# Seven block products instead of eight in four last blocks, with GpSimd making low parts of streamed operands

## The chip, the cores and the metric

The kernel runs on one core of one Trainium2 chip. The metric is the device time of one execution, in microseconds; lower is better. TensorE (PE) multiplies matrices, VectorE (DVE), ScalarE (ACT) and GpSimd (POOL) work on tiles, and SyncE (SP) issues most DMA transfers.

## What is computed

One layer of a streaming encoder on a sequence of 2048 tokens of width 1024, in float32: token mixing, cross-attention into 256 memory tokens, and a dense SwiGLU feed-forward with 2816 hidden channels, each between root-mean-square norms and with a residual. The part around the change is the last:

```python
u = rms_norm(h, g_ffn_pre[l])
y = (jax.nn.silu(u @ w_gate[l]) * (u @ w_up[l])) @ w_down[l]
h = h + rms_norm(y, g_ffn_post[l])
```

## The kernel before, in words

Every float32 factor is split into a high part (a copy rounded to the matmul's type `F32R`) and a low part (the rest), and a product of two factors is three matmuls: high by high, high by low, low by high (`products`, lines 1122 to 1124). `split2` makes the two parts: ScalarE (line 985) or GpSimd (line 987) copies the high part, VectorE subtracts to get the low part (line 988).

The large products after the mixing are a list of jobs (`jobs`, line 1411), run one after the other by `phases` (line 1210): the output projection, the two products of the cross-attention, the feed-forward for the first and for the second half of the tokens (22 blocks each: gate and up in turn), and the down projection in three jobs of 8 blocks over 6, 8 and 8 of the 22 hidden tiles. A job has one *resident* factor, kept in SBUF for all its blocks, and a *streamed* factor that is loaded per block. Each block is a 2 x 2 block matrix product. Kind `s` does it in seven block products in Strassen's manner (`seven`, steps 1, 5, 6, 3, 7, 2, 4), kind `p` in eight plain ones (`eight`, resident blocks 1, 2, 8, 3, two products each). A block product is 3 x nk matmuls of 128 x 512; nk is 4, and 3 in the first down job. In the seven-product form the resident factor comes as seven tiles (blocks and sums of blocks; the sums are made ahead and lie in DRAM as `u_s` and `d_s`), and the streamed factor as seven operands of 128 x 512, four of them sums made by VectorE (`combine`, line 1097). Products 1, 5 and 6 of a block are copied out of PSUM by ScalarE (`copy`, line 1137) and added to later ones by VectorE in the block's `out`.

SBUF has seven places for resident tiles (`slots` in `phases`: four called A, three called B). A resident tile is made in two halves, each loaded into one of nine row buffers (`row_tile`, line 1453; `half` issues the load) and split two steps later (`split`: ScalarE the high part, VectorE the low part; these instructions are queued behind the last ScalarE and VectorE work of the step, by `behind`). A place can be reused after the last product that reads it. In each step of an `s` block the loop of `phases` does one `split` and one `half`; in each step of a `p` block (four steps, two products each) it does two of both. With a last block of kind `p`, the places of 5, 7, 6 and 4 are free from the block before it on; an eighth tile, key 8, is needed for the `p` block itself.

Streamed operands have five buffers (tag `S`) and are made two steps ahead in the order of the code (`upto`). In the feed-forward and down jobs ScalarE makes all their high parts. In the second and third down job the partial sums of the rows are added from DRAM by accumulating transfers that GpSimd issues (`add`, line 1500).

The order of instructions on each engine is set when the program is built: a scheduler takes the instructions in the order of the code, by when it expects them to be ready, and may put products of the next block ahead of one whose operand is late. On the chip the queues then run in that order.

Of the kernel before, what the change touches and what calls it, by code (L numbers as in the profile page):

```python
# [15 lines left out]
ALU = mybir.AluOpType  # L16
AX = mybir.AxisListType

P = 128
# [6 lines left out]
NFF = DFF // P  # L26
# [3 lines left out]
NT = T // P  # L30
# [6 lines left out]
def f32(ap):  # L37
    return ap.bitcast(F32)
# [10 lines left out]
class Layer:  # L49
# [89 lines left out]
    def split(self, raw, hi, lo, engine="P"):  # L139

        self.split2(raw, hi, lo, engine)
# [837 lines left out]
    TAKES = {"s": (1,) * 7, "p": (2, 2, 0, 0), "q": (4, 0), "u": (2, 2), "v": (0, 0)}  # L979
    BLOCK = {1: (0, 0), 8: (0, 1), 2: (1, 0), 3: (1, 1)}  # L980

    def split2(self, raw, hi, lo, engine):

        if engine == "A":
            self.nc.scalar.activation(hi, raw, AF.Copy)  # L985
        else:
            self.nc.gpsimd.tensor_scalar(hi, raw, 1.0, 1.0, ALU.mult, ALU.mult)  # L987
        self.nc.vector.tensor_tensor(lo, raw, f32(hi), ALU.subtract)  # L988

    CHAIN = (5, 7, 6, 4)  # L990

# [68 lines left out]
        for e in (mybir.EngineType.Activation, mybir.EngineType.DVE):  # L1060
            self.last[e] = next((i for i in reversed(traced) if i.engine == e), None)

    def streamed(self, load, nk, kind, engine=None, tiles=False):


        nc = self.nc
        raw = []
        for j in range(2):
            self._n += 1
            t = self.ts.tile([P, 4, 256], F32, tag="raw", name=f"sraw_{self._n}", bufs=self.raws)  # L1070
            if tiles:
                t = t.rearrange("p k c -> p (k c)").rearrange("p (i c) -> p i c", i=2)
                load(t, j)
                raw.append([t[:, i, :].rearrange("p (k c) -> p k c", k=4) for i in range(2)])
            else:
                t = t[:, :nk, :]
                load(t, j)
                raw.append([t[:, :, i * P:(i + 1) * P] for i in range(2)])
        yield None
        (a11, a21), (a12, a22) = raw  # L1080

        room = []
        if kind == "u":
            t = self.tb.tile([P, 4, 2, 4, P], F32R, tag="T", name="S_u", bufs=3)
            room += [t[:, i] for i in range(4)]

        def made(src, e):
            self._n += 1
            t = room.pop(0) if room else self.ts.tile([P, 2, 4, P], F32R, tag="S", name=f"S_{self._n}", bufs=5)
            t = t[:, :, :nk, :]  # L1090
            self.split2(src, t[:, 0], t[:, 1], engine or e)
            return t

        def combine(a, b, op):
            self._n += 1
            t = self.st_pool.tile([P, 4, P], F32, tag="sum", name=f"sum_{self._n}", bufs=3)[:, :nk, :]
            nc.vector.tensor_tensor(t, a, b, op)
            return t

        if kind in "pqu":  # L1100
            for a, e in ((a11, "P"), (a21, "A"), (a12, "P"), (a22, "P")):
                yield made(a, e)
            return
        yield made(a11, "A")
        s1 = combine(a21, a22, ALU.add)
        yield made(s1, "P")
        s2 = combine(s1, a11, ALU.subtract)
        yield made(s2, "A")
        yield made(combine(a12, s2, ALU.subtract), "A")
        yield made(combine(a11, a21, ALU.subtract), "P")  # L1110
        yield made(a12, "A")
        yield made(a22, "P")
# [97 lines left out]
    def phases(self, jobs, first, prologue=None):  # L1210
# [117 lines left out]
        g = 0  # L1328
        at = 0
        self.last = {}  # L1330
        for _, nk, bl, _, beside in jobs:
            for i, (kind, _, out, follow, addend) in enumerate(bl):
                stream(at + 1)
                after += [f() for f in beside.get(i, ())]
                run = (self.seven(ready, Ready(), nk, out, addend) if kind == "s" else
                       self.eight(ready, Ready(), nk, out) if kind == "p" else
                       self.plain(ready, Ready(), nk, out, addend, kind))
                for q in range(len(self.STEPS[kind])):
                    for _ in range(1 if g or not first else 3):
                        next(run)  # L1340
                        if first and g < 3:
                            yield
                    self.mark()
                    upto(need[g + 2])
                    if first and g == 1:
                        yield
                    for _ in range(1 if kind == "s" else 2):
                        for f in list(after):
                            if next(f, after) is after:
                                after.remove(f)  # L1350
                        if pending and lag(pending[0][1]):
                            with self.behind():
                                split(g)
                        else:
                            split(g)
                        if not first or g > 1:
                            half(g, self.row_tile)
                    g += 1
                after.append(follow())
                at += 1  # L1360
        for f in after:
            for _ in f:
# [48 lines left out]
    def jobs(self):  # L1411
# [7 lines left out]
        def ffn_u(b):  # L1419
            return lambda t, i, j, k0, n: self.load(  # L1420
                t, self.u_d[4 * i + k0:4 * i + k0 + n, :, b * TB + j * 512:b * TB + (j + 1) * 512]
                .rearrange("k p t -> p k t"))

        def kinds(blocks, n=0):
            return [("p" if i < n or i == len(blocks) - 1 else "s",) + b for i, b in enumerate(blocks)]

        def sums(name, src, nk, other=None):
            return self.sums(name, src, nk, self.extra_tile, other or self.gain_tile)
# [12 lines left out]
                (vo, 4, kinds([self.value_block(n) for n in range(0, NT, 2)]), vo_s[0], {})]  # L1441
        for b in range(NB):
            beside = {2: [in_turn(*(d[1] for d in d_s))]} if b else {4: [u_s[1]]}
            jobs.append((ffn_u(b), 4, kinds([blk for f in range(0, NFF, 2) for blk in self.hidden_blocks(b, f)]),
                         u_s[0] if b else self.u0_s, beside))
        for c, (src, f0, nk) in enumerate(down):
            jobs.append((src, nk, kinds([self.down_block(c, f0, nk, n) for n in range(0, NT, 2)]), d_s[c][0], {}))
        k, s, o, f, a = jobs[-1][2][-1]
        jobs[-1][2][-1] = ("s", s, o, f, a)

        return jobs

# [171 lines left out]
    def hidden_blocks(self, b, f):  # L1624
        nc = self.nc
        act = {}

        def stream(w):
            return lambda kind: self.streamed(lambda t, j: self.load(
                t, w[j * 512:(j + 1) * 512, f * P:(f + 2) * P].rearrange("(k p) c -> p k c", p=P)), 4, kind, "A")  # L1630

        def gate(i, j, a, c):
            if i not in act:
# [19 lines left out]
        def nothing():  # L1653
            return iter(())

        return [(stream(self.I["w_gate"]), gate, nothing, None), (stream(self.I["w_up"]), up, nothing, None)]

    def down_block(self, c, f0, nk, n):
        nc = self.nc
# [5 lines left out]
        def stream(kind):  # L1665
            if late:
                for i in range(2):
                    y[i] = self.rows_of(self.y2_d, n + i)
            if last and n == 0:
                self.g_post = self.gain(self.I["g_ffn_post"])  # L1670
            return self.streamed(lambda t, j: self.load(
                t, self.h_d[f0 + j * nk:f0 + (j + 1) * nk, :, n * P:(n + 2) * P].rearrange("k p t -> p k t")),
                nk, kind, "A")

        def part(i, j):
            return y[i][:, j * 512:(j + 1) * 512]
# [78 lines left out]
```

## Time and profile before

| what | value |
|---|---|
| device time of three runs | 2588.64, 2589.82, 2592.41 us (median 2589.82) |
| span of the profiled execution, first to last instruction | 2585.7 us |
| PE busy | 2548.3 us, 99% of the span |
| DVE, ACT, POOL busy | 1747.9, 1261.0, 428.4 us |
| granted TensorE clock, mean | 0.998 |

The profiled execution has no device time of its own on the page beside its span; the span is 4.1 us under the median of the runs, which is the time outside the first and last instruction together with the scatter. In the rows of groups, the numbers after the first bar are the busy time of the group in us and the mean of one instruction in ns; after the second bar stands the engine's idle time just before those instructions, with what ended it. In rows of the timeline the first number is the start, the second the duration, both in us, and a bracket holds the idle time before with what ended it. Matmuls overlap in the pipeline, so their listed durations add up to more than the time they fill.

In time, the first feed-forward job ends at about 1728 us, the second at 2150, the first down job at 2266 and the second at 2421.

### The profile page before, as it was taken

Reading aid. Unit: us, or ns where it says so; the run is one execution under the profiler, and the core shown is the slowest. Engines: PE = TensorE matmul, PEld = TensorE weight load, DVE = VectorE, ACT = ScalarE, POOL = GpSimd, SP = SyncE. Lnnn points to the kernel's source line nnn. Section 1 sums busy time; section 2 is a strip of 40 time slices with the busy share of each in tenths; the row PEclk is TensorE's granted clock in tenths of the full one; section 3 lists DMA queues with packets and bytes.
Section 4 is the critical chain, followed back from the end, with each engine's and each line's share of the span. In section 5 each row is a group of like instructions: output and inputs, shape, how many; then the busy total and the mean of one; then the engine's idle time right before and its main releaser. Section 6 shows DMA issues by size and latency. Waiting matters only on the chain.

```text
span 2585.7 us, 34998 instructions
## 1 busy us (share of the span) xinstructions
PE 2548.3 (99%) x12371; PEld 2135.9 (83%) x12371; DVE 1747.9 (68%) x2759; ACT 1261.0 (49%) x2633; POOL 428.4 (17%) x612
## 2 busy tenths in 40 slices
PE   9999999999999999999999999999999999999998
PEld 8888888888988778888878888888888888888886
DVE  7785588986557778788876655576566556564656
ACT  5563466665555566465563333353333334443543
POOL 5231334321302232222300000000000000000022
PEclk9999999999999999999999999999999999999999
DMA  6445655855888886666963622253565444566888
GB/s 188 147 163 179 198 168 152 253 185 167 258 290 281 296 287 210 205 222 210 327 233 115 203 97 75 98 203 124 177 205 194 146 146 139 208 201 186 262 213 218
DMA packets 363663, 506.03 MB, mean 196 GB/s; under 512 B 20960, under 2 KB 249312, under 8 KB 363488
## 3 DMA queue, kind: packets, MB, share of 16 engines
q1 hardware_dynamic: 357440, 481.77, 56.5%
q0 software_dynamic: 6048, 22.02, 4.7%
q8 instruction: 97, 1.59, 0.2%
q14 instruction: 78, 0.64, 0.1%
HBM read 337.00 MB, written 166.72 MB: 195 GB/s over the span
## 4 chain that ended last, share of the span: by engine, by line
PE 83%; DMA 7%; DVE 4%; ACT 3%; issue 2%; POOL 1%; SPq 0%; DVEq 0%; POOLq 0%; ACTq 0%
PE psm L1122 23%; PE psm L1124 23%; PE psm L1123 22%; PE psg L156 2%; PE psg L157 2%; PE psg L158 2%; PE pss L1374 1%; DMA row<-y_d 1%; DMA raw<-in_wo_x_dram 1%; DMA u_d<-row 1%; DMA h1t_d<-row 1%; DMA row<-h_d 1%; ACT junk L1471 1%; ACT T L985 0%; PE pss L837 0%
## 5 line engine op out<-in xcount | busy, mean ns | idle before, releaser
L1122 PE MATMUL psm<-T,S 128*128 128x512 f32 x2695 | 1043.8, 391 | 11.0 <-ACT part L1137 6.5
L1123 PE MATMUL psm<-T,S 128*128 128x512 f32 x2695 | 1049.1, 390 | 2.1 <-DVE T L988 1.9
L1124 PE MATMUL psm<-T,S 128*128 128x512 f32 x2695 | 1038.9, 390 | 3.6 <-DVE S L988 3.6
L1122 PEld LDWEIGHTS psm<-T,S 128*128 128x128 f32 x2695 | 506.2, 188 | 120.3 <-ACT part L1137 7.0
L1124 PEld LDWEIGHTS psm<-T,S 128*128 128x128 f32 x2695 | 506.2, 188 | 110.4 <-DVE S L988 5.3
L1123 PEld LDWEIGHTS psm<-T,S 128*128 128x128 f32 x2695 | 506.5, 188 | 107.5 <-DVE T L988 4.1
L985 ACT ACTIVATE S<-sum 128x512 fp32r<-128x512 f32 (+1 forms) x314 | 188.7, 619 | 359.6 <-PE psm L1124 267.8
L988 DVE TENSOR_TENSOR S<-sraw,S 128x512 fp32r<-128x512 f32 (+1 forms) x319 | 217.0, 687 | 215.9 <-ACT S L985 201.8
L988 DVE TENSOR_TENSOR S<-sum,S 128x512 fp32r<-128x512 f32 (+1 forms) x372 | 249.7, 681 | 47.0 <-ACT S L985 31.8
L1137 ACT ACTIVATE part<-psm 128x512 f32<-128x512 f32 x273 | 161.7, 597 | 242.8 <-PE psm L1124 221.5
L985 ACT ACTIVATE S<-sraw 128x512 fp32r<-128x512 f32 (+1 forms) x272 | 167.4, 617 | 111.2 <-PE psm L1124 99.3
L1500 POOL DMA_DIRECT2D row<-y_d x28 | 25.7, 919 | 1111.4 <-DVE row L1686 1036.5
L988 DVE TENSOR_TENSOR T<-row,T 128x1024 fp32r<-128x1024 f32 (+1 forms) x120 | 141.3, 1192 | 60.9 <-ACT T L985 60.4
L1471 ACT ACTIVATE junk<-row 128x512 f32<-128x512 f32 x160 | 99.7, 625 | 60.5 <-DVE row L1493 30.0
L157 PE MATMUL psg<-u,whi 128*128 128x512 f32 x320 | 127.8, 399 | 0.0
L158 PE MATMUL psg<-u,wlo 128*128 128x512 f32 x320 | 127.1, 397 | 0.0
L156 PE MATMUL psg<-u,whi 128*128 128x512 f32 x320 | 127.1, 397 | 0.0
L985 ACT ACTIVATE T<-row 128x1024 fp32r<-128x1024 f32 x120 | 119.9, 1028 | 10.5 <-DMA row<-qk_s 3.5
L987 POOL TENSOR_SCALAR S<-sum 128x512 fp32r<-128x512 f32 x58 | 53.4, 921 | 294.6 <-PE psm L1124 237.2
L1637 DVE TENSOR_TENSOR row<-psm,part 128x512 f32<-128x512 f32 x66 | 43.7, 687 | 61.4 <-PE psm L1124 61.3
L1646 DVE TENSOR_TENSOR part<-psm,part 128x512 f32<-128x512 f32 x60 | 39.7, 687 | 62.4 <-PE psm L1124 62.2
L812 ACT ACTIVATE S<-S,w_mn 128x256 f32<-128x256 f32 (+1 forms) x128 | 63.1, 495 | 28.6 <-DVE w_mn L808 28.3
(363 smaller groups left out, 3679.1 us busy)
## 6 DMA issues: line engine op xcount, KB each, us to landing
sraw<-in_w_gate_dram SPq DMA_DIRECT2D x44, 512.0 KB, 3.7
sraw<-in_w_up_dram SPq DMA_DIRECT2D x44, 512.0 KB, 3.7
hid_d<-row SPq DMA_DIRECT2D x44, 512.0 KB, 2.7
h_d<-row SPq DMA_DIRECT2D x32, 512.0 KB, 4.8
y_d<-row SPq DMA_DIRECT2D x32, 512.0 KB, 3.3
sraw<-hid_d SPq DMA_DIRECT2D x32, 512.0 KB, 5.1
row<-y_d POOLq DMA_DIRECT2D x28, 512.0 KB, 7.1
sraw<-in_w_in_dram SPq DMA_DIRECT2D x44, 256.0 KB, 3.5
```

Of the source, the lines that this page charges most:

```text
L156: nc.tensor.matmul(ps, ah, bh, start=(i == 0), stop=False)
L157: nc.tensor.matmul(ps, ah, bl, start=False, stop=False)
L158: nc.tensor.matmul(ps, al, bh, start=False, stop=(i == n - 1))
L812: nc.scalar.activation(s[:, r, o:], s[:, r, o:], AF.Exp, bias=mn[:, i:i + 1], scale=-1.0, accum_out=den[:, i:i + 1])
L985: self.nc.scalar.activation(hi, raw, AF.Copy)
L987: self.nc.gpsimd.tensor_scalar(hi, raw, 1.0, 1.0, ALU.mult, ALU.mult)
L988: self.nc.vector.tensor_tensor(lo, raw, f32(hi), ALU.subtract)
L1122: nc.tensor.matmul(ps, s[:, 0, k, :], t[:, 0, k, :], start=st, stop=False, **kw)
L1123: nc.tensor.matmul(ps, s[:, 0, k, :], t[:, 1, k, :], start=False, stop=False, **kw)
L1124: nc.tensor.matmul(ps, s[:, 1, k, :], t[:, 0, k, :], start=False, stop=sp, **kw)
L1137: nc.scalar.activation(t, ps, AF.Copy)
L1471: self.nc.scalar.activation(junk, a, AF.Square, scale=float(D) ** -0.5, accum_out=to)
```

## The change

The last blocks of both feed-forward jobs and of the first two down jobs become kind `s` (the last block of the third down job had that kind already). In such a last block, and in the first block of the job behind it, each step does a second `split`; in the last block the first, fourth and seventh step also do a second `half`. The second `split` isn't queued behind the step's other work. For the blocks on both sides of each of these four operand changes, GpSimd makes the low parts of the streamed operands, by the same subtraction that VectorE did; the low parts of the resident operand stay on VectorE.

```diff
@@ -979,13 +979,13 @@
     TAKES = {"s": (1,) * 7, "p": (2, 2, 0, 0), "q": (4, 0), "u": (2, 2), "v": (0, 0)}
     BLOCK = {1: (0, 0), 8: (0, 1), 2: (1, 0), 3: (1, 1)}
 
-    def split2(self, raw, hi, lo, engine):
+    def split2(self, raw, hi, lo, engine, by_pool=False):
 
         if engine == "A":
             self.nc.scalar.activation(hi, raw, AF.Copy)
         else:
             self.nc.gpsimd.tensor_scalar(hi, raw, 1.0, 1.0, ALU.mult, ALU.mult)
-        self.nc.vector.tensor_tensor(lo, raw, f32(hi), ALU.subtract)
+        (self.nc.gpsimd if by_pool else self.nc.vector).tensor_tensor(lo, raw, f32(hi), ALU.subtract)
 
     CHAIN = (5, 7, 6, 4)
 
@@ -1060,7 +1060,7 @@
         for e in (mybir.EngineType.Activation, mybir.EngineType.DVE):
             self.last[e] = next((i for i in reversed(traced) if i.engine == e), None)
 
-    def streamed(self, load, nk, kind, engine=None, tiles=False):
+    def streamed(self, load, nk, kind, engine=None, tiles=False, lo=False):
 
 
         nc = self.nc
@@ -1088,7 +1088,7 @@
             self._n += 1
             t = room.pop(0) if room else self.ts.tile([P, 2, 4, P], F32R, tag="S", name=f"S_{self._n}", bufs=5)
             t = t[:, :, :nk, :]
-            self.split2(src, t[:, 0], t[:, 1], engine or e)
+            self.split2(src, t[:, 0], t[:, 1], engine or e, lo)
             return t
 
         def combine(a, b, op):
@@ -1328,6 +1328,7 @@
         g = 0
         at = 0
         self.last = {}
+        fresh = False
         for _, nk, bl, _, beside in jobs:
             for i, (kind, _, out, follow, addend) in enumerate(bl):
                 stream(at + 1)
@@ -1335,6 +1336,7 @@
                 run = (self.seven(ready, Ready(), nk, out, addend) if kind == "s" else
                        self.eight(ready, Ready(), nk, out) if kind == "p" else
                        self.plain(ready, Ready(), nk, out, addend, kind))
+                change = kind == "s" and i == len(bl) - 1
                 for q in range(len(self.STEPS[kind])):
                     for _ in range(1 if g or not first else 3):
                         next(run)
@@ -1355,8 +1357,13 @@
                             split(g)
                         if not first or g > 1:
                             half(g, self.row_tile)
+                    if change or kind == "s" and fresh:
+                        split(g)
+                        if change and q in (0, 3, 6):
+                            half(g, self.row_tile)
                     g += 1
                 after.append(follow())
+                fresh = change
                 at += 1
         for f in after:
             for _ in f:
@@ -1421,8 +1428,8 @@
                 t, self.u_d[4 * i + k0:4 * i + k0 + n, :, b * TB + j * 512:b * TB + (j + 1) * 512]
                 .rearrange("k p t -> p k t"))
 
-        def kinds(blocks, n=0):
-            return [("p" if i < n or i == len(blocks) - 1 else "s",) + b for i, b in enumerate(blocks)]
+        def kinds(blocks, n=0, last="p"):
+            return [("p" if i < n else last if i == len(blocks) - 1 else "s",) + b for i, b in enumerate(blocks)]
 
         def sums(name, src, nk, other=None):
             return self.sums(name, src, nk, self.extra_tile, other or self.gain_tile)
@@ -1441,12 +1448,10 @@
                 (vo, 4, kinds([self.value_block(n) for n in range(0, NT, 2)]), vo_s[0], {})]
         for b in range(NB):
             beside = {2: [in_turn(*(d[1] for d in d_s))]} if b else {4: [u_s[1]]}
-            jobs.append((ffn_u(b), 4, kinds([blk for f in range(0, NFF, 2) for blk in self.hidden_blocks(b, f)]),
+            jobs.append((ffn_u(b), 4, kinds([blk for f in range(0, NFF, 2) for blk in self.hidden_blocks(b, f)], 0, "s"),
                          u_s[0] if b else self.u0_s, beside))
         for c, (src, f0, nk) in enumerate(down):
-            jobs.append((src, nk, kinds([self.down_block(c, f0, nk, n) for n in range(0, NT, 2)]), d_s[c][0], {}))
-        k, s, o, f, a = jobs[-1][2][-1]
-        jobs[-1][2][-1] = ("s", s, o, f, a)
+            jobs.append((src, nk, kinds([self.down_block(c, f0, nk, n) for n in range(0, NT, 2)], 0, "s"), d_s[c][0], {}))
 
         return jobs
 
@@ -1625,9 +1630,10 @@
         nc = self.nc
         act = {}
 
-        def stream(w):
+        def stream(w, lo):
             return lambda kind: self.streamed(lambda t, j: self.load(
-                t, w[j * 512:(j + 1) * 512, f * P:(f + 2) * P].rearrange("(k p) c -> p k c", p=P)), 4, kind, "A")
+                t, w[j * 512:(j + 1) * 512, f * P:(f + 2) * P].rearrange("(k p) c -> p k c", p=P)), 4, kind, "A",
+                lo=lo)
 
         def gate(i, j, a, c):
             if i not in act:
@@ -1653,7 +1659,8 @@
         def nothing():
             return iter(())
 
-        return [(stream(self.I["w_gate"]), gate, nothing, None), (stream(self.I["w_up"]), up, nothing, None)]
+        return [(stream(self.I["w_gate"], b == 1 and f == 0), gate, nothing, None),
+                (stream(self.I["w_up"], f == NFF - 2), up, nothing, None)]
 
     def down_block(self, c, f0, nk, n):
         nc = self.nc
@@ -1670,7 +1677,7 @@
                 self.g_post = self.gain(self.I["g_ffn_post"])
             return self.streamed(lambda t, j: self.load(
                 t, self.h_d[f0 + j * nk:f0 + (j + 1) * nk, :, n * P:(n + 2) * P].rearrange("k p t -> p k t")),
-                nk, kind, "A")
+                nk, kind, "A", lo=n == 0 or n == NT - 2 and not last)
 
         def part(i, j):
             return y[i][:, j * 512:(j + 1) * 512]
```

## The prediction

> **What bounds the kernel now.** I read the page's head first, for the engine that has no room, and then the groups of instructions in the stretch where all four operand changes lie (1687 to 2440 us).
>
> ```profile
> span 2585.7 us, 34998 instructions
> PE 2548.3 (99%) x12371; PEld 2135.9 (83%) x12371; DVE 1747.9 (68%) x2759; ACT 1261.0 (49%) x2633; POOL 428.4 (17%) x612
> PEclk9999999999999999999999999999999999999999
> ```
>
> TensorE is busy throughout and its granted clock stays in the top tenth. The groups of the stretch, with the idle time ahead of each after the second bar:
>
> ```profile
> L1123 PE MATMUL psm<-T,S 128*128 128x512 f32 x1108 | 430.2, 389 | 0.0
> L1122 PE MATMUL psm<-T,S 128*128 128x512 f32 x1108 | 425.8, 389 | 0.0
> L1124 PE MATMUL psm<-T,S 128*128 128x512 f32 x1107 | 425.7, 389 | 0.0
> L985 ACT ACTIVATE S<-sum 128x512 fp32r<-128x512 f32 (+1 forms) x148 | 87.6, 609 | 180.5 <-PE psm L1124 132.3 <-issue 48.2
> L1137 ACT ACTIVATE part<-psm 128x512 f32<-128x512 f32 x111 | 66.4, 598 | 114.8 <-PE psm L1124 103.1 <-issue 10.3 <-DVE S L988 0.7
> L985 ACT ACTIVATE T<-row 128x1024 fp32r<-128x1024 f32 x64 | 61.7, 1002 | 4.2 <-DMA row<-in_w_down_dram 2.2 <-DMA row<-d_s 1.9
> L1097 DVE TENSOR_TENSOR sum<-sraw,sum 128x512 f32<-128x512 f32 (+1 forms) x37 | 24.6, 665 | 1.1
> L1648 DVE TENSOR_TENSOR row<-part,row 128x512 f32<-128x512 f32 x31 | 21.2, 683 | 0.0
> L1500 POOL DMA_DIRECT2D row<-y_d x16 | 14.0, 877 | 1080.2 <-DVE row L1686 1018.8 <-ACT row L1690 39.4 <-DMA y_d<-row 11.2
> ```
>
> PE's idle time is 0.0 here, so the number of matmuls sets the time. A matmul is listed with 389 ns, but they overlap: 3323 of them fill 753 us, one each 0.2266 us, and that is what one less is worth. Last, the work of each engine in the four last blocks (first, third, fourth and sixth row) and in three of the blocks after them:
>
> ```profile
> core 0: us, PE busy (x) PEld busy (x) DVE busy (x) ACT busy (x) POOL busy (x), PEclk, DMA share, GB/s
> 1706.30:1728.00 21.70, 21.70 (x97) 17.99 (x96) 14.70 (x17) 11.04 (x14) 0.00 (x0) 1.00 0.90 328
> 1728.10:1747.00 18.90, 18.90 (x85) 15.66 (x84) 15.80 (x19) 11.71 (x18) 0.00 (x0) 1.00 0.41 132
> 2127.90:2149.60 21.70, 21.70 (x97) 17.99 (x96) 12.15 (x17) 8.70 (x14) 0.00 (x0) 1.00 0.67 234
> 2249.60:2265.90 16.30, 16.30 (x73) 13.51 (x72) 9.54 (x12) 9.00 (x13) 0.00 (x0) 1.00 1.00 354
> 2266.00:2285.00 19.00, 19.00 (x86) 15.72 (x85) 18.51 (x25) 13.77 (x19) 0.24 (x1) 1.00 0.69 242
> 2399.20:2420.90 21.70, 21.70 (x97) 17.97 (x96) 12.40 (x15) 9.23 (x13) 1.72 (x2) 1.00 1.01 322
> 2421.00:2440.00 19.00, 19.00 (x85) 15.75 (x84) 14.81 (x19) 13.76 (x19) 0.87 (x1) 1.00 0.87 274
> ```
>
> VectorE is the engine next to the bound: 18.51 of 19.00 us in the block after the third change, still with PE full. GpSimd does almost nothing. So the question is whether the preparation of the next resident operand still fits when the last block is shorter.
>
> **What is removed on PE.** A block of kind p has eight products of 3 x nk matmuls, one of kind s has seven. Four blocks lose one: 12 (nk 4) in each feed-forward job, 9 (nk 3) in the first down job, 12 in the second, 45 in all. 45 x 0.2266 = 10.2 us. This is on the path in full, PE being idle 0.0 before. A step of s lasts 12 x 0.2266 = 2.72 us, or 2.04 us with nk 3; a last block shrinks from 21.7 to 19.0 us, the first down job's from 16.3 to 14.3.
>
> **What else goes or comes.** Each of the four jobs needs no eighth resident operand: two loads, two ScalarE high parts (1.00 us each) and two VectorE low parts fewer. A last block gets three more streamed high parts (0.61), three copies (0.60) and four sums (0.67). On ScalarE that is 3.6 - 2.0 = 1.6 us more, at most 12.6 us of 19.0: nothing, covered by PE's own 19 us, and 1.6 us per change without cover. The seven streamed low parts of the last block and of the one behind it go from VectorE to GpSimd, 56 in all.
>
> **What tightens.** An s block uses all seven resident tiles, so a new operand can be written only after the old one's last product, in the same order. Following the code, the 14 halves of the new operands now come up at the ends of 11 steps, from the third of the last block (five steps) to the sixth of the next (six). Before, 16 halves were spread from the second-last block on. The row of VectorE for such a half, and how GpSimd prices its own work:
>
> ```profile
> 958.66 2.35 DVE L988 TENSOR_TENSOR T<-row,T 128x1024 fp32r<-128x1024 f32 x2
> 524.41 1.21 DVE L1032 TENSOR_TENSOR x<-x,u 128x1024 f32<-128x1024 f32 x1
> ```
>
> ```profile
> 523.34 1.03 POOL L877 TENSOR_TENSOR qq<-qq,G 128x256 f32<-128x256 f32 x1 [6.48 <-DMA qq<-z_d]
> 524.33 2.20 POOL L889 TENSOR_TENSOR q<-qq,G 128x512 f32<-128x512 f32 x1
> 526.49 0.61 POOL L877 TENSOR_TENSOR qq<-qq,G 128x256 f32<-128x256 f32 x1
> 527.06 1.04 POOL L889 TENSOR_TENSOR q<-qq,G 128x512 f32<-128x512 f32 x1
> ```
>
> Two halves back to back take 2.35 us, 1.18 each. No subtract of this shape ran on GpSimd before; the nearest row, also two inputs and 512 columns, took 1.04 us. But the same instruction took 2.20 us at 524.33, when VectorE's L1032, with both inputs in SBUF, began 0.08 us later: GpSimd finished 0.91 us after it. So a GpSimd instruction and a VectorE one with two SBUF inputs don't run side by side, and moving a low part moves work to another engine without moving it off what the two share. In VectorE's favour is only what reads PSUM.
>
> The ledger of the shared time over the 11 steps: low halves 14 x 1.18 = 16.5; five sums x 0.66 = 3.3; three products of L1648 in an up block, 2.0; eleven streamed low parts on GpSimd x 1.04 = 11.4 (for nk 3 I take 0.83, half way from 0.61 at 256 columns to 1.04; its resident halves 7 x (1.18 + 0.68) = 13.0).
> Feed-forward 0 to 1: 33.2 us of work in 11 x 2.72 = 29.9, short by 3.3.
> Feed-forward 1 to down 0: 13.0 + 3.3 + 2.0 + 3 x 1.04 + 8 x 0.83 = 28.1 in 5 x 2.72 + 6 x 2.04 = 25.8, short by 2.3.
> Down 0 to 1: 16.5 + 3.3 + 3 x 0.83 + 8 x 1.04 = 30.6 in 5 x 2.04 + 6 x 2.72 = 26.5, short by 4.1.
> Down 1 to 2: 16.5 + 3.3 + 11.4 = 31.2 in 29.9, short by 1.3.
> Together 11.0 us, which is the upper price; the lower is 0. Not below it: nothing waits on PE now that could be won. A shortfall need not reach PE, as this row shows:
>
> ```profile
> 1752.87 1.23 DVE L988 TENSOR_TENSOR T<-row,T 128x1024 fp32r<-128x1024 f32 x1 [0.62 <-ACT T L985]
> ```
>
> That is the last of the 16 halves of the second feed-forward's operand; it came 5.9 us after seven products' time (1747.0) had passed, and PE never waited: it had taken products of the next block first. The streamed operands have room as well: ScalarE's high parts wait 132.3 us for PE to free their five buffers, so they run ahead as far as these allow. I take a third of the 11.0, 3.7 us, nearer to the row of 18.51 us busy without a wait than to full price, but not nothing, since a queue order fixed in advance holds no reserve on an engine pair that takes turns.
>
> The Trainium skill's GPSIMD Engine Reference, section Engine selection, calls GpSimd about twice as slow as VectorE on two-input elementwise work, which speaks against the move. The trace has 1.04 against 0.68, a factor of 1.5. By the page, as an estimate, a low part would take 1.36 us, the shortfalls would be some 13 us larger, a third of that 4 us more, and the time 2587.6.
>
> **Queues.** On GpSimd the new low parts stand in line with the accumulating stores of L1500 in the second and third down job (0.88 us each, two to a block). Those wait for VectorE's L1686, and low parts queued behind wait too; with the rows done by the end of the block before and 1.04 + 0.88 us inside a 2.72 us step I put it at 0, at most one step. On SP three half loads move up in each last block.
>
> **Sum.** 2589.8 (the median) - 10.2 + 3.7 = **2583.3 us**. In the profiled execution: 2585.7 - 6.5 = 2579.2 us of span; the 4.1 us between span and median stay.
>
> **Rivals.** *The pair takes it all.* If GpSimd and VectorE exclude each other with no gain from reordering, all 11.0 us reach PE: 2589.8 - 10.2 + 11.0 = 2590.6. For it: 2.20 against 1.04 us. Against it: the late half that cost nothing.
> The Trainium skill's SBUF — State Buffer, section Who interferes with whom, states the same as a rule: a VectorE instruction with two SBUF inputs and a GpSimd one that reads SBUF block each other for a whole instruction. The 524.33 row agrees.
>
> *Late rows, and slower.* The operand's halves pass through nine row buffers from DRAM, 512 KB each:
>
> ```profile
> row<-u_d SPq DMA_DIRECT2D x20, 512.0 KB, 6.0
> row<-d_s SPq DMA_DIRECT2D x20, 512.0 KB, 8.2
> y_d<-row SPq DMA_DIRECT2D x32, 512.0 KB, 3.3
> ```
>
> Ten halves, two streamed tiles and two stores, 14 x 0.524 = 7.3 MB, now belong to a last block. Down 0's has 14.3 us; at the 354 GB/s of its row, DMA share 1.00, they take 20.7. What that does is seen where an earlier job changed operands:
>
> ```profile
> 961.08 1.06 ACT L985 ACTIVATE T<-row 128x1024 fp32r<-128x1024 f32 x1 [3.10 <-DMA row<-qk_s]
> 965.94 1.06 ACT L985 ACTIVATE T<-row 128x1024 fp32r<-128x1024 f32 x1 [2.80 <-DMA row<-qk_d]
> ```
>
> ```profile
> 959.93 0.50 PE L1123 MATMUL psm<-T,S 128*128 128x512 f32 x1 [0.92 <-DVE T L988]
> 962.76 0.47 PE L1122 MATMUL psm<-T,S 128*128 128x512 f32 x1 [1.41 <-ACT part L1137]
> 967.04 0.73 PE L1122 MATMUL psm<-T,S 128*128 128x512 f32 x2 [2.45 <-ACT T L985]
> ```
>
> ScalarE, in order, sits on a row that has not landed, its copies of PSUM queue behind, and PE loses 0.92 + 1.41 + 2.45 = 4.8 us. Four such changes cost 19.1 us: 2598.7. It decides from 10.2 / 4 = 2.6 us per change. Against it: the same DMA share of 1.00 and 1.01 in two of the four last blocks now, without a wait; loads aren't tied to a step and there are two fewer per change.
>
> *The change does less than it says:* PE's order was full already, so the blocks would have to remain eight products; 2589.8. The code leaves little doubt that they don't.
>
> **Chances and range.** Forecast, PE losing under 5 us in all: 0.50. The pair takes 5 to 15 us: 0.28. Late rows: 0.19, slower by over 0.2% in all of it. No effect: 0.03. 0.2% is 5.2 us, about what a measurement of this kernel can tell from none. The forecast's own range is 2579.6 (no loss) to 2584.6 (5 us lost), all faster; the second and fourth count as the same, 0.31. The range reaches from 2579.0, the full gain and some scatter, to 2596.0, where the second case and part of the third lie inside.
>
> **What would show it.** Right: 45 psm matmuls fewer; 56 GpSimd TENSOR_TENSORs of 1.0 to 2 us; PE idle of 2 to 5 us in all, on VectorE's T or GpSimd's S, in the blocks after the changes, most after down 0. The pair: VectorE halves stretched from 1.2 towards 1.6 to 2.2 us and about 11 us of PE idle. Late rows: ScalarE's T idle on DMA, PE on copies. Wrong altogether: PE idle elsewhere, or the matmul's pace no longer 0.2266 us.

## The result and the profile after

The changed kernel takes 2598.13 us (median of 10 runs), the kernel before on the same chip 2592.8 us (10 runs): ratio 1.0019, 95% interval 1.0010 to 1.0028. It is slower by some 5 us (4.9 by the ratio, 5.3 by the medians), where 6.5 us faster was forecast. The profiled execution took 2598.83 us, of which 2597.1 us are span.

The head of the profile page of the changed kernel:

```profile
span 2597.1 us, 34970 instructions
...
PE 2546.0 (98%) x12326; PEld 2130.9 (82%) x12326; DVE 1756.2 (68%) x2735; ACT 1261.3 (49%) x2643; POOL 510.1 (20%) x668
...
PEclk9999999999999999999999999999999999999999
```

PE has 12326 matmuls instead of 12371: the 45 are gone. GpSimd has 56 instructions more, and VectorE is as busy as before (1756.2 against 1747.9 us) though it has 24 instructions fewer. The groups of the stretch with the four operand changes:

```profile
L1123 PE MATMUL psm<-T,S 128*128 128x512 f32 x1153 | 449.2, 391 | 5.4 <-DVE T L988 5.4
L1122 PE MATMUL psm<-T,S 128*128 128x512 f32 x1154 | 443.5, 390 | 5.4 <-ACT part L1137 5.4
...
L988 DVE TENSOR_TENSOR T<-row,T 128x1024 fp32r<-128x1024 f32 (+1 forms) x56 | 74.7, 1356 | 31.5 <-ACT T L985 31.5
...
L985 ACT ACTIVATE T<-row 128x1024 fp32r<-128x1024 f32 (+1 forms) x56 | 55.7, 1005 | 22.5 <-DMA row<-in_w_down_dram 11.1 <-DMA row<-d_s 9.5 <-DMA row<-u_d 0.9
L988 POOL TENSOR_TENSOR S<-sum,S 128x512 fp32r<-128x512 f32 (+1 forms) x32 | 47.8, 1507 | 31.8 <-ACT S L985 28.8 <-DVE row L1643 2.9
L988 POOL TENSOR_TENSOR S<-sraw,S 128x512 fp32r<-128x512 f32 (+1 forms) x24 | 35.9, 1496 | 869.0 <-ACT S L985 868.8
```

PE, which had no idle time here, now has 10.8 us: half behind VectorE's low parts of T (a tile of the resident operand), half behind ScalarE's copies out of PSUM. It never waits for GpSimd's S (a streamed operand) itself. A low part of S takes GpSimd 1.50 us in the mean, where the prediction had 1.04. ScalarE waits 22.5 us for rows of T (before: 4.2). By stage, the four changes one under the other:

```profile
core 0: us, PE busy (x) PEld busy (x) DVE busy (x) ACT busy (x) POOL busy (x), PEclk, DMA share, GB/s
1690.00:1780.00 90.00, 88.00 (x386) 72.10 (x386) 60.69 (x74) 44.63 (x69) 22.14 (x14) 1.00 0.49 170
2110.00:2180.00 70.00, 67.99 (x301) 55.95 (x300) 47.77 (x67) 33.86 (x59) 17.81 (x14) 1.00 0.50 175
2230.00:2300.00 70.00, 67.34 (x292) 54.23 (x291) 47.94 (x57) 37.41 (x60) 23.20 (x16) 1.00 0.67 226
2390.00:2460.00 70.00, 65.87 (x281) 54.02 (x280) 43.31 (x46) 35.17 (x54) 28.16 (x21) 0.95 0.80 245
sum 300.00, PE 289.19 PEld 236.30 DVE 199.71 ACT 151.07 POOL 91.30; mean PE 72.30 PEld 59.08 DVE 49.93 ACT 37.77 POOL 22.83
```

Every change loses something, the last most. Idle time understates it: a listed matmul ends after the next could have started, and the last row's clock is 0.95. So I count a stop as the distance between the starts of two psm matmuls less 0.2267 us, and add those up around each change:

| us lost around | ff 0 to 1 | ff 1 to down 0 | down 0 to 1 | down 1 to 2 | sum | sum less matmuls saved | measured (interval) |
|---|---|---|---|---|---|---|---|
| changed kernel | 2.65 | 2.29 | 4.04 | 6.66 | 15.6 | +5.4 | +4.9 (2.6 to 7.3) |
| after_again | 2.67 | 2.27 | 3.89 | 5.33 | 14.2 | +4.0 | +5.2 (1.8 to 8.6) |
| lows_on_dve | 1.33 | 0 | 1.18 | 2.74 | 5.3 | -4.9 | -11.7 (-15.6 to -7.8) |
| dve_again | 1.34 | 0 | 1.43 | 2.59 | 5.4 | -4.8 | -8.3 (-11.7 to -4.9) |
| write_only | 0.96 | 1.00 | 1.44 | 3.52 | 6.9 | -3.3 | -5.4 (-8.6 to -2.3) |
| dve_light | 0.96 | 1.51 | 0.45 | 1.11 | 4.0 | -6.2 | -5.4 (-8.3 to -2.9) |
| store_pool | 1.34 | 0 | 1.77 | 2.63 | 5.7 | -4.5 | -7.5 (-10.1 to -4.7) |
| no_acc | 1.33 | 0 | 2.19 | 0.11 | 3.6 | -6.6 | -9.3 (-12.5 to -6.5) |
| ffn_dve | 1.34 | 0 | 0 | 0 | 1.3 | -4.1 | -5.4 (-8.6 to -2.6) |
| pool_only | 0 | 0 | 0.65 | 0 | 0.7 | +0.7 | -0.3 (-3.1 to +2.3) |

In the kernel before all four are 0. The last two columns are in us against the kernel before; the measured one is the ratio less one, times some 2595 us. The runs are told below. The count covers the four changes alone: after 2460 us, near the end of the kernel, the kernel before loses another 3.1 us, the changed one 6.2, and its repeat 2.8. The kernel before itself gave 2588.9 to 2601.9 us over the 27 runs beside one group of these kernels, so one execution's count and a median can differ by a few us.

### The profile page after: what moved, and what is told of

Same layout as the page of the kernel before. It is cut to its first block, busy times and chain, and to the rows that moved or that the text cites. A ratio compares the mean times of both kernels' runs of the same rounds, so it can differ in the third digit from the quotient of the medians.

```text
span 2597.1 us, 34970 instructions
## 1 busy us (share of the span) xinstructions
PE 2546.0 (98%) x12326; PEld 2130.9 (82%) x12326; DVE 1756.2 (68%) x2735; ACT 1261.3 (49%) x2643; POOL 510.1 (20%) x668
## 4 chain that ended last, share of the span: by engine, by line
PE 80%; DMA 7%; DVE 5%; issue 3%; ACT 3%; POOL 2%; SPq 0%; DVEq 0%; POOLq 0%; ACTq 0%
PE psm L1123 21%; PE psm L1122 21%; PE psm L1124 21%; PE psg L158 2%; PE psg L157 2%; PE psg L156 2%; PE pss L1381 1%; DMA row<-y_d 1%; DVE T L988 1%; DMA row<-h_d 1%; DMA u_d<-row 1%; ACT T L985 1%; DMA y_d<-sg 1%; ACT junk L1476 1%; DMA x<-in_w_out_dram 0%
## 5 line engine op out<-in xcount | busy, mean ns | idle before, releaser
L1122 PE MATMUL psm<-T,S 128*128 128x512 f32 x2680 | 1038.6, 392 | 17.3 <-ACT part L1137 11.8
L985 ACT ACTIVATE S<-sum 128x512 fp32r<-128x512 f32 (+1 forms) x330 | 198.5, 618 | 372.8 <-PE psm L1124 265.2
L988 DVE TENSOR_TENSOR S<-sraw,S 128x512 fp32r<-128x512 f32 (+1 forms) x291 | 198.1, 690 | 200.5 <-ACT S L985 184.9
L1137 ACT ACTIVATE part<-psm 128x512 f32<-128x512 f32 x285 | 168.6, 596 | 230.3 <-PE psm L1124 213.1
L988 DVE TENSOR_TENSOR S<-sum,S 128x512 fp32r<-128x512 f32 (+1 forms) x356 | 240.3, 683 | 48.4 <-ACT S L985 32.6
L988 POOL TENSOR_TENSOR S<-sraw,S 128x512 fp32r<-128x512 f32 (+1 forms) x24 | 35.9, 1496 | 869.0 <-ACT S L985 868.8
L985 ACT ACTIVATE T<-row 128x1024 fp32r<-128x1024 f32 (+1 forms) x112 | 113.7, 1030 | 26.5 <-DMA row<-in_w_down_dram 11.1
L1643 DVE TENSOR_TENSOR row<-psm,part 128x512 f32<-128x512 f32 x66 | 43.7, 687 | 72.6 <-PE psm L1124 72.6
L1693 DVE TENSOR_TENSOR row<-psm,part 128x512 f32<-128x512 f32 x72 | 49.0, 687 | 52.0 <-PE psm L1124 49.3
```

The source lines that it names most:

```text
L988: (self.nc.gpsimd if by_pool else self.nc.vector).tensor_tensor(lo, raw, f32(hi), ALU.subtract)
L1122: nc.tensor.matmul(ps, s[:, 0, k, :], t[:, 0, k, :], start=st, stop=False, **kw)
L1137: nc.scalar.activation(t, ps, AF.Copy)
L1693: nc.vector.tensor_tensor(d, a, b, ALU.add)
```

## The experiments

Three theories were set against each other: (A) *the pair*: GpSimd's subtract shuts VectorE out and VectorE's low parts of T come late; (B) *late rows*: the rows of the next operand land late; (C) the second `split` costs more than it brings.

**lows_on_dve.** All low parts back on VectorE, the rest as changed:

```diff
-        (self.nc.gpsimd if by_pool else self.nc.vector).tensor_tensor(lo, raw, f32(hi), ALU.subtract)
+        self.nc.vector.tensor_tensor(lo, raw, f32(hi), ALU.subtract)
```

> The change without GpSimd: the low parts of the streamed operands stay on VectorE, the four last blocks stay at seven products. Theory of the pair (GpSimd and VectorE shut each other out; the changed kernel's S low takes 1.29 us undisturbed and up to 2.28 beside VectorE, T lows up to 2.32): all T lows are back at 1.2 us, VectorE's own work over the 11 steps is short of time by some 12 us in the four changes instead of 21, PE loses some 5 to 10 us there instead of 15.6, and the time is 0 to 5 us under before (ratio 0.998 to 1.000). Theory of late rows (the loads of the operand's halves come too late): the rows are the same, PE loses 13 to 18 us as in the changed kernel, ratio 1.001 to 1.003.

Ratio 0.9955 (0.994 to 0.997), faster than either theory had it: 2588.05 against 2595.67 us. Its groups in the same stretch and the sum of its four windows:

```profile
L1122 PE MATMUL psm<-T,S 128*128 128x512 f32 x1169 | 448.8, 390 | 3.2 <-ACT part L1137 1.9 <-DVE row L1693 1.1 <-ACT T L985 0.2
...
L988 DVE TENSOR_TENSOR T<-row,T 128x1024 fp32r<-128x1024 f32 (+1 forms) x56 | 63.8, 1152 | 13.0 <-ACT T L985 13.0
L985 ACT ACTIVATE T<-row 128x1024 fp32r<-128x1024 f32 (+1 forms) x56 | 55.8, 1006 | 17.3 <-DMA row<-in_w_down_dram 8.0 <-DMA row<-d_s 7.8 <-DMA row<-u_s 0.9
```

```profile
sum 300.00, PE 296.75 PEld 243.26 DVE 213.67 ACT 153.18 POOL 6.90; mean PE 74.19 PEld 60.81 DVE 53.42 ACT 38.30 POOL 1.72
```

The wait on VectorE's T is gone and T's low parts are back from 1356 to 1152 ns. For about the same work VectorE and GpSimd together are listed busy 220.6 us here and 291.0 us in the changed kernel; the 70 us between are GpSimd's slower subtract and the time in which one of the two stands shut out. This takes away 10.3 of the 15.6 us lost (8.8 of 14.2 between the repeats of both kernels): A is the main part, and 5.3 us remain that are something else.

**write_only.** GpSimd writes the low part without reading:

```diff
-        (self.nc.gpsimd if by_pool else self.nc.vector).tensor_tensor(lo, raw, f32(hi), ALU.subtract)
+        if by_pool:
+            self.nc.gpsimd.memset(f32(lo), 0.0)
+        else:
+            self.nc.vector.tensor_tensor(lo, raw, f32(hi), ALU.subtract)
```

> As the change, but GpSimd writes zeros (memset) into the streamed low parts of those blocks instead of subtracting: it writes as much, reads no SBUF, and the low parts are left out of the result. Theory of the pair, of reading: no T low over 1.3 us, PE loses under 4 us in the four changes, time 6 to 10 us under before (ratio 0.996 to 0.998). If writing alone shuts VectorE out: T lows still stretched beyond 1.5 us. Theory of late rows: PE loses 10 to 16 us as in the change, ratio about 1.001.

Ratio 0.9979 (0.9967 to 0.9991).

```profile
L991 DVE TENSOR_TENSOR T<-row,T 128x1024 fp32r<-128x1024 f32 (+1 forms) x56 | 63.6, 1153 | 41.2 <-ACT T L985 41.2
...
L989 POOL MEMSET S<- 128x512 f32 (+1 forms) x56 | 28.3, 508 | 943.4 <-PE psm L1127 934.3 <-issue 7.4 <-ACT T L985 1.7
```

56 instructions of GpSimd into the same tiles, at the same places in the order, and VectorE's T takes 1153 ns as it does alone. 14 of the 56 low parts of T run at the same time as one of GpSimd's writes, and none takes over 1.23 us; in the changed kernel 27 overlap a subtract of GpSimd and take 1.57 us in the mean, up to 2.32. So what shuts VectorE out is GpSimd's reading, not its writing. The Trainium skill's SBUF — State Buffer, section Who interferes with whom, says so (a GpSimd instruction that only writes doesn't contend with a VectorE one with two SBUF inputs); this trace agrees, 1153 against 1356 ns. What the shorter instruction (0.51 against 1.50 us) contributes to the 8.7 us won is not separated; PE's waits were on T and the copies, not on S. PE still loses 6.9 us, more than the 4 expected for A and less than the 10 for B.

**one_split** and **dve_one_split.** The changed kernel, and the one with low parts on VectorE, without these lines:

```diff
-                    if change or kind == "s" and fresh:
-                        split(g)
-                        if change and q in (0, 3, 6):
-                            half(g, self.row_tile)
```

> The change without the second split and the extra half loads: GpSimd and seven products stay. Theory of the pair: the same work shares the same ports and comes later in the order, so PE loses at least as much as in the change, 15 to 30 us; ratio 1.002 to 1.008. Theory of late rows: fewer loads crowd into the last block, ScalarE's T waits less on DMA, PE loses under 10 us; ratio 0.999 to 1.001.

> Seven products in the four last blocks, all low parts on VectorE, and neither the second split nor the extra half loads. With GpSimd on, taking these out cost some 26 us. If that cost came from the pair (operands late because GpSimd and VectorE take turns), it shrinks here to under 8 us: ratio 0.995 to 1.000. If it came from the later place of the loads and splits in the order alone, it stays: PE loses 15 us or more, ratio 1.002 to 1.008.

1.0121 (1.0105 to 1.0137) and 1.0109 (1.0090 to 1.0129). PE's groups, first of one_split, then of dve_one_split:

```profile
L1123 PE MATMUL psm<-T,S 128*128 128x512 f32 x1117 | 440.1, 394 | 17.9 <-DVE T L988 17.9
...
L1122 PE MATMUL psm<-T,S 128*128 128x512 f32 x1118 | 432.6, 393 | 6.6 <-ACT T L985 6.6
```

```profile
L1123 PE MATMUL psm<-T,S 128*128 128x512 f32 x1123 | 441.0, 393 | 11.2 <-DVE T L988 11.2
...
L1122 PE MATMUL psm<-T,S 128*128 128x512 f32 x1123 | 433.8, 393 | 11.8 <-ACT T L985 11.8
```

PE waits for T itself, 24.5 and 23.0 us, whichever engine makes the low parts of S: one half per step comes up too late for an operand that can be written only as its places come free. C falls: the second `split`, with the loads that go with it, is what makes seven products pay. The count from 1690 to 2500 us (the later stops fall outside the windows above) gives about 40 and 37 us lost, +30 and +27 us net, near the measured +31 and +28. That is more than any of the theories had expected; the cost stays without GpSimd, as the second expectation says it does if the place in the order makes it.

**pool_only.** The other part alone: the blocks stay of kind `p`, GpSimd makes the low parts (44 here, since a `p` block streams four operands, not seven):

```diff
-                change = kind == "s" and i == len(bl) - 1
+                change = False
...
-            jobs.append((src, nk, kinds([...], 0, "s"), d_s[c][0], {}))
+            jobs.append((src, nk, kinds([...], 0, "s" if c == 2 else "p"), d_s[c][0], {}))
```

(and `kinds` of the feed-forward jobs without `"s"`).

> The kernel before (eight products in the four last blocks, one split and one half per step) with only the low parts of the streamed operands around the four operand changes moved to GpSimd. Theory of the pair: T lows of up to 2.3 us appear, and PE, which lost nothing there before, loses 3 to 12 us; ratio 1.001 to 1.005. Theory of late rows: loads are those of before, PE loses under 1 us; ratio 1.000.

0.9999 (0.9988 to 1.0009).

```profile
L1123 PE MATMUL psm<-T,S 128*128 128x512 f32 x1176 | 456.6, 389 | 0.4 <-DVE T L988 0.4
...
L988 DVE TENSOR_TENSOR T<-row,T 128x1024 fp32r<-128x1024 f32 (+1 forms) x64 | 80.8, 1287 | 32.3 <-ACT T L985 32.3
...
L988 POOL TENSOR_TENSOR S<-sraw,S 128x512 fp32r<-128x512 f32 (+1 forms) x28 | 43.2, 1550 | 885.7 <-ACT S L985 880.7 <-DVE row L1643 3.1 <-issue 1.1
```

The two engines hold each other up here as well (T 1287 ns, S 1550 ns), and yet PE loses 0.7 us. By the expectation that is the outcome of late rows: the pair alone doesn't stop PE here. A likely reason, not tested, is that with a last block of kind `p` the halves of T are spread over more steps. Seven products alone lose 5.3 us, GpSimd's low parts alone 0.7, both on the same steps 15.6.

**after_again.** The changed kernel once more, unchanged.

> The change once more, beside the runs below on one chip. If the first comparison holds, ratio 1.001 to 1.003, PE losing 13 to 18 us in the four operand changes.

1.0020 (1.0007 to 1.0033), and 2.67, 2.27, 3.89 and 5.33 us lost: the first three changes repeat within 0.15 us, the last varies.

**store_pool.** lows_on_dve, with the stores of the partial sums moved off SP's queue, where they stand behind the accumulating transfers and ahead of row loads:

```diff
-                    self.store(self.y2_d[(n + i) * P:(n + i + 1) * P, :], y[i])
+                    q = nc.gpsimd if c else nc.sync
+                    q.dma_start(self.y2_d[(n + i) * P:(n + i + 1) * P, :], y[i])
```

> Low parts on VectorE, two splits per step, and the stores of the second down job's partial sums issued by GpSimd instead of SP, so that SP, in order, no longer stands behind an accumulating transfer (10.8 us at the third change) with the operand's loads queued behind. Theory of late rows for what is left: ScalarE's T waits for DMA less, PE's loss at the last change falls from 2.7 to under 1 us; ratio 0.994 to 0.997. If what is left is VectorE being full: loss unchanged, ratio as without.

0.9971 (0.9961 to 0.9982); the last change loses 2.63 us, before 2.74. By the expectation this speaks for a full VectorE; but ScalarE still stands 10.2 us there before rows of T (9.8 in lows_on_dve), so the edit didn't bring the rows any earlier and doesn't decide between the two. What it shows is that the place of these stores in SP's line is not what makes rows late. (The transfer of 10.8 us that the expectation names stands at the last change.)

**ffn_dve.** lows_on_dve with only the two feed-forward jobs' last blocks in seven products (the edit of the down jobs is that of pool_only).

> Only the two feed-forward last blocks at seven products, low parts on VectorE, two splits; the down jobs as before. 24 matmuls fewer, 5.4 us; at these two changes PE lost 1.3 us without GpSimd: 4 us under before, ratio 0.998 to 0.999. If the four changes are alike and each gains, this gains less than all four.

0.9979 (0.9967 to 0.9990): with 24 matmuls saved (5.4 us) and 1.3 us lost. By the count, the down jobs' 21 matmuls (4.8 us) are worth little more than the 3.9 us that their two changes lose in lows_on_dve; the ratios of that kernel (0.9955 and 0.9968) put them somewhat higher.

**dve_again, dve_light, no_acc.** lows_on_dve again; the same with zeros written by VectorE in place of the low parts that GpSimd makes in the changed kernel; the same without the second down job's additions and stores:

```diff
+        if by_pool:
+            self.nc.vector.memset(f32(lo), 0.0)
+        else:
             self.nc.vector.tensor_tensor(lo, raw, f32(hi), ALU.subtract)
```

```diff
-                if c:
+                if c and c != 1:
                     self.add(y[i], self.y2_d, n + i)
-                if not last:
+                if not last and c != 1:
                     self.store(self.y2_d[(n + i) * P:(n + i + 1) * P, :], y[i])
```

> The kernel with all low parts on VectorE once more, unchanged, because its first comparison (11.6 us faster) and the count of its stops in the operand changes (10.2 us of matmuls saved, 5.3 us lost again, so some 5 us faster) do not meet. If the count is right: ratio 0.9975 to 0.9985, and 5 to 6 us lost in the changes. If the comparison was right: ratio about 0.9955, and the profile has to show some 5 us won outside the four changes.

> All low parts on VectorE, but the streamed ones of the last blocks and the blocks behind them are written as zeros there instead of being subtracted (those low parts are left out of the products). This takes away part of VectorE's 0.68 us for each of the 56. If the 5.3 us that PE still loses with the low parts on VectorE come from VectorE being full, PE loses under 2.5 us in the changes and the ratio is 0.9965 or below. If they come from the rows of the next operand that land late, PE still loses 4 to 6 us, ScalarE's T still stands 15 us or more idle on the DMA, and the ratio stays that of the kernel with all low parts on VectorE.

> All low parts on VectorE, and the second down job adds nothing to the partial sums of the first and stores none (its sums are left out of the result). So near the last change two accumulating loads and two stores of 512 KB in each block are gone, and a row buffer is free as soon as it is written. If late rows hold the last change: its loss falls from 2.7 us to under 1 us, and ScalarE's T idle on the DMA there from 9.8 us to under 4. If VectorE being full holds it: the loss stays at 2 to 3 us. The changes before it (1.3, 0 and 1.2 us) stay as they are in both cases; the whole is faster by another 0 to 3 us.

dve_again: 0.9968 (0.9955 to 0.9981), 2588.17 against 2595.47 us, 5.4 us lost again. The interval (down to -4.9 us) now ends next to the count (-4.8). That the first comparison had 6.8 us more than the count stays open; some 2 us of it are the kernel's end (1.1 to 1.4 us lost after 2460 us, before 3.1).

dve_light: 0.9979 (0.9968 to 0.9989), 4.0 us lost, at the lower edge of what B gives and above the 2.5 us of a full VectorE, while ScalarE's wait for rows fell to 11.9 us, under the 15 that B gives. A zero written takes 458 ns in the mean where the subtract takes some 664, so little is taken off VectorE, and the run decides nothing by itself. At the last change, though, the loss fell from 2.7 to 1.1 us, which suggests that VectorE's load has a share there too. At the second change it rose from 0 to 1.5 us, which stays open.

no_acc: 0.9964 (0.9952 to 0.9975). The last change's window, and ScalarE's rows of T from 2390 to 2450 us, lows_on_dve first:

```profile
2390.00:2460.00 70.00, 67.91 (x298) 55.40 (x297) 47.14 (x63) 35.46 (x56) 5.23 (x7) 1.00 0.87 256
...
L985 ACT ACTIVATE T<-row 128x1024 fp32r<-128x1024 f32 x14 | 14.8, 1059 | 9.8 <-DMA row<-in_w_down_dram 5.1 <-DMA row<-d_s 4.7
```

```profile
2390.00:2460.00 70.00, 70.00 (x310) 57.66 (x309) 50.56 (x67) 37.80 (x62) 5.75 (x8) 1.00 0.60 184
...
L985 ACT ACTIVATE T<-row 128x1024 fp32r<-128x1024 f32 x14 | 14.8, 1062 | 2.7 <-DMA row<-d_s 1.5 <-DMA row<-in_w_down_dram 1.2
```

DMA share 0.60 for 0.87, ScalarE's wait 2.7 for 9.8 us, PE's loss 0.11 for 2.7 us: with these transfers gone the last change loses next to nothing, with VectorE as busy as ever (50.6 us), so late rows (B) are what holds it, though by dve_light a lighter VectorE may ease it too. Whether the transfers' share or the row buffers that they hold is the limit wasn't separated. The third change was to stay at 1.2 us and lost 2.2, which stays open. Of the 1.3 us of the first change, 0.85 are neither A nor B. Of lows_on_dve's timeline:

```profile
1741.20 0.39 PE L1124 MATMUL psm<-T,S 128*128 128x512 f32 x1
1741.63 0.60 ACT L1137 ACTIVATE part<-psm 128x512 f32<-128x512 f32 x1 [0.44 <-PE psm L1124]
1742.28 0.50 PE L1122 MATMUL psm<-T,S 128*128 128x512 f32 x1 [0.69 <-ACT part L1137]
```

ScalarE stands idle until PE has ended a product, copies it, and PE waits for this copy. The same stop, 0.85 us, is in all nine runs that have seven products and the second `split` at this change, the changed kernel too.

So lows_on_dve beats the kernel before, 0.9955 and 0.9968 in two comparisons, where the changed kernel is slower than it (1.0019 and 1.0020); store_pool, 0.9971, likewise.

## Why the prediction was wrong

**Removed on PE:** right. 45 matmuls fewer at a pace of 0.2270 us, 10.2 us.

**Cost of a GpSimd low part:** the first step that failed. Its row (1.04 us) belonged to another instruction, a product whose second factor is repeated along the columns, with an f32 result. Of the changed kernel's timeline, undisturbed ones, then two that alternate with VectorE, with PE's stops beside them:

```profile
1715.26 1.30 POOL L988 TENSOR_TENSOR S<-sraw,S 128x512 fp32r<-128x512 f32 x1 [3.30 <-ACT S L985]
1717.21 1.29 POOL L988 TENSOR_TENSOR S<-sraw,S 128x512 fp32r<-128x512 f32 x1 [0.65 <-ACT S L985]
...
2275.66 6.82 DVE L988 TENSOR_TENSOR T<-row,T 128x1024 fp32r<-128x1024 f32 x4
2275.92 4.34 POOL L988 TENSOR_TENSOR S<-sraw,S 128x512 fp32r<-128x512 f32 x2 [3.27 <-ACT S L985]
...
2279.16 0.50 PE L1123 MATMUL psm<-T,S 128*128 128x512 f32 x1 [0.58 <-DVE T L988]
2281.39 0.50 PE L1123 MATMUL psm<-T,S 128*128 128x512 f32 x1 [0.58 <-DVE T L988]
```

Alone it takes 1.29 us (and 1.02 with nk 3, not 0.83). The estimate from the Trainium skill's GPSIMD Engine Reference, section Engine selection, was 1.36: there the Trainium skill was nearer than the row chosen. The ledger with 1.29 and 1.02 is short by 6.1, 4.5, 6.7 and 4.1 us, 21 instead of 11.0.

**A third of it reaches PE:** the second step that failed. In the first three changes 9.0 us were lost against 17.3 of this ledger, half. Four halves of T, 4.8 us alone, lasted 6.82 us at 2275.66 with two of GpSimd's between them, and PE stood twice for T in that time. The late half at 1752.87, on which the third leaned, was late in a block with reserve: in pool_only, with eight products, the low parts of T are stretched as well and cost 0.7 us, and with seven products they cost PE far more.

**The rivals.** The pair's signs came: T's low parts stretched (from 1.15 to 1.36 us in the mean, single ones to 2.32), and about 11 us of PE idle. But it was priced at no more than its ledger, and the last change lost 6.7 us against 4.1. There the chain is the other rival's, as the timeline shows:

```profile
2430.67 0.39 PE L1124 MATMUL psm<-T,S 128*128 128x512 f32 x1
2431.65 1.06 ACT L985 ACTIVATE T<-row 128x1024 fp32r<-128x1024 f32 x1 [5.76 <-DMA row<-in_w_down_dram]
...
2434.55 0.59 ACT L1137 ACTIVATE part<-psm 128x512 f32<-128x512 f32 x1
...
2435.19 0.80 PE L1122 MATMUL psm<-T,S 128*128 128x512 f32 x1 [4.13 <-ACT part L1137]
```

ScalarE stands 5.76 us before a row that hasn't landed, the copy out of PSUM is queued behind it, and PE waits for the copy. Why the row was late, the same timeline shows in VectorE's and SP's instructions:

```profile
2416.52 1.21 SPq L75 DMA_DIRECT2D row<-d_s  x2
2418.80 1.77 DVE L1097 TENSOR_TENSOR sum<-sraw 128x512 f32<-128x512 f32 x1 [0.59 <-POOL S L988]
2420.60 0.37 SPq L75 DMA_DIRECT2D sraw<-hid_d  x1
2421.07 1.04 SPq L75 DMA_DIRECT2D row<-in_w_down_dram  x2
```

The row that ScalarE waits for landed at 2431.62 and is the second load of the last line. SP issues it behind a load of a streamed tile, and that load had to wait until VectorE's sum ended at 2420.57. The sum was held up by GpSimd's low parts: it started behind one and took 1.77 us instead of 0.68. So SP stood some 2.9 us, and the repeat of the changed kernel shows the same wait for the same sum; in lows_on_dve the two loads of `w_down` (2415.75) follow the two of `d_s` (2414.31) without a stop. The forecast had put the queues at 0, at most one step of 2.72 us. How much of the 4.5 us stop comes of this wait wasn't measured; the transfers were at a DMA share of 1.03 as well.

Both rivals were given as alternatives; here both act: 10.3 of the 15.6 us go with GpSimd's low parts, some 5 stay without them, and the last change, where rows are late, loses more where the pair is slow as well (6.7 against 2.7 us). "Late rows, and slower" had the time nearly right (2598.7), with the smaller cause.

**Where it would be lost:** "most after down 0" was wrong; the row of 18.51 us counted VectorE alone and not the transfers. Whether the copies' extra 1.6 us on ScalarE cost nothing by themselves, as forecast, wasn't tested.

**The sum.** In short, two steps of the forecast failed: the ledger was mis-sized (21 us short, not 11.0), and the share of it that reaches PE was put at a third, with late rows and queues at nothing beside it, where 15.6 us were lost instead of 3.7. The 10 runs of the kernel before beside the changed one have a median of 2592.8 us, 3.0 above the 2589.8 that the prediction started from. 2592.8 - 10.2 + 15.6 = 2598.2, measured 2598.13; that this meets to 0.1 us is luck, since the count is of one execution, varies (14.2 in the repeat), and leaves out the end of the kernel. Of the 14.8 us of error, 3.0 are the base and 11.9 the loss (15.6 instead of 3.7).

## What to carry to other kernels

Work moved from VectorE to GpSimd is not off VectorE when both read two SBUF operands: as far as this kernel shows (GpSimd's writes alone did no harm), enter it in VectorE's own ledger at GpSimd's duration (here 1.29 us for 0.69), and move it only where that ledger has room. When the bound engine's stage gets shorter, what must be prepared inside it has to begin earlier or twice as densely (the second `split` with its loads was worth some 26 us with GpSimd's low parts and 37 to 40 without), and then the transfers come next. When two rivals rest on the same scarce reserve, price their sum, not each alone.

## What was not expected of the hardware

In the stop of 4.5 us at 2430.67, the clock granted to TensorE fell to half:

```profile
2425.00:2435.00 10.00, 6.06 (x27) 4.69 (x25) 5.12 (x4) 4.24 (x7) 4.04 (x4) 0.91 1.03 383
2435.00:2440.00 5.00, 4.81 (x11) 3.85 (x12) 5.00 (x4) 5.00 (x8) 3.61 (x2) 0.50 0.92 265
2440.00:2450.00 10.00, 10.00 (x45) 8.23 (x44) 10.00 (x14) 5.50 (x8) 0.00 (x0) 0.99 0.52 187
```

After the stop 11 matmuls went at 0.43 us each, then the clock was back: 2.2 us on top of the stop, a third of the last change's loss. A shorter stop near the end did the same:

```profile
2548.93 0.39 PE L1124 MATMUL psm<-T,S 128*128 128x512 f32 x1
2552.56 0.58 PE L1122 MATMUL psm<-T,S 128*128 128x512 f32 x1 [3.23 <-DVE part L1139]
2552.94 0.63 PE L1123 MATMUL psm<-T,S 128*128 128x512 f32 x1
2553.36 0.63 PE L1124 MATMUL psm<-T,S 128*128 128x512 f32 x1
```

The starts before and after it are 3.6 us apart, the next ones 0.4 us. A stop of 2.4 us between starts (2155.88 to 2158.28) showed no fall: the next matmul came 0.34 us later and those behind it 0.23 apart. The Trainium skill's TensorE: Matmul & The Clock Gate, section What's actually happening, puts the fall at an idle window of about 3.4 us and the return at about as much busy time. This trace agrees with the two figures in the main: the stops of 3.6 and 4.5 us have a fall, that of 2.4 us has none, and by finer windows the clock stood at half for some 3.4 us with the 3.6 us stop (2552.8 to 2556.2) and 6.8 us with the other (2433.3 to 2440.1). But the length of the stop alone doesn't decide. At 2430.67 the clock was 1.00 from 2430 to 2433 and 0.65 from 2433 to 2434, so it fell 2.6 us after the last start; and in one_split a stop of 2.4 us (1744.05 to 1746.44), behind one of 0.85, did bring a fall (0.50 from 1747 to 1750), while three of 2.1 to 2.5 us between 2170 and 2182 had none. So the price of a stop isn't linear: in these traces stops from some 2.4 us on may cost about 2 us more at once.
